# Reordering four places of a planned kernel: a conformer and state-space hybrid step on one Trainium2 core

## Chip, cores, metric

The kernel runs on one core of a Trainium2 chip. Times are device microseconds of one execution, from the first to the last work of the program; the median of several runs is compared. All arithmetic is in 32 bits.

## What is computed

One decoder layer for 2048 prompt tokens and 8 sample tokens, D = 1024. Cut to what the change bears on:

```
h = rmsnorm(x, g_pre);  proj = h @ w_in          # c_a c_b c_z | s_x s_z | g_c g_s
u = c_a * sigmoid(c_b);  v = causal_depthwise_conv(u, K=31)
v = silu(layernorm(v)) * silu(c_z);   y_c = v @ w_pc
ys = gelu(ssm(s_x));  ys = ys * sigmoid(ys @ w_glu + b_glu) * silu(s_z);  y_s = ys @ w_ps
o = (sigmoid(g_c) * y_c + sigmoid(g_s) * y_s) @ w_out
x1 = x + rmsnorm(o, g_post)
y = x1 + rmsnorm(p @ w_ple, g_ple) * sigmoid(x1 @ w_pg + b_pg)
```

The state-space branch (ssm) needs its discretisation first: dt = exp(log_dt) and exp(a_re * dt), for 128 x 16 parameters.

## The kernel before

Channels lie on the 128 partitions, tokens on the free axis. The tokens are worked in two halves: half 0 has 1032 columns (1024 prompt tokens and 8 samples, in blocks of 344), half 1 has 1024 (blocks of 512). A tile of a half is 128 channels; eight tiles are one activation.

Every product of a weight matrix is made of three matmuls: both operands are split into a high and a low part (names ending in h and l, for weights whi and wlo), and the products high-high, high-low and low-high are summed in one PSUM bank (`stages`, L310 to L312). The high part is a cast on ScalarE (L360, weights L263), the low part a subtraction on VectorE or GpSimd (L353). A weight chunk is 128 x 1024 and serves 128 to 512 outputs; its load (SP's queue, two raw buffers), cast and split (GpSimd) run one chunk ahead. The order of the chunks is the list `order` (L225 to L245).

A half goes through these stages (function `half`, L1142): s_x chunks; u chunks (c_b then c_a) with the gates in between; s_z; w_glu, evacuated by ScalarE's sigmoid; w_ps, whose result VectorE multiplies by the gate gs from DRAM; eight chunks of c_z (`act_to(z, AF.Silu)`, L1435); w_pc; w_out in two column parts; w_pg in two column parts. Beside them run tasks: the convolution on VectorE, partly on ScalarE and GpSimd; the state-space scans; the LayerNorm (`ln_task`, L1236); after w_glu the split of ys into ynh and ynl (`ysn_task`, L1394), which w_ps reads.

The order of instructions on each engine is fixed when the program is built. `Background` (L31) keeps an estimated clock for TensorE (`pe`) and for VectorE, ScalarE and GpSimd ("V", "S", "G"). A task is a generator: before each step it yields an engine and the time at which its operand is ready. `pump` emits the steps that may begin before `pe`: the earliest first, and the better priority (the lower number) among those within 0.05 us. An emitted step is one unit that the others can't enter, and `use` advances its engine's clock by its estimated cost. `drain` and `until` go on emitting beyond `pe` until a condition holds. A step on "P" (TensorE) counts as ready 1.2 us after its operand, a step on "Q" another MARGIN = 9.0 us later (L26, L60, L66).

The places that the change touches:

- `exp_dve` (L458): the exponential in 15 small VectorE operations of 128 x 16. `ssm_setup` (L475, priority 6) makes one copy, the first exponential, a product and the second, in one step that is booked with 11.0 us (L492 to L496). The tiles of h of the second column part of half 0 (`h_tile_task`, L724, from L1113, priority -1.7) become ready when `h_part`'s norm is done (L1106).
- `mean_task` (L369) and `norm_task` (L414): a column mean as a product with a matrix of 1/D. The sum is split (nh, nl), multiplied on TensorE (L385, L386) and evacuated by ScalarE (L396 or L398). `late=True` asks for "Q"; the LayerNorm's two calls (L1262, L1274) and `rms_task` (L1056) do so.
- the LayerNorm waits with its centring for `back_task` (L1188), which is added after w_ps (L1433) and loads six v tiles back from DRAM; `ln_out` (L1216) multiplies by cz and splits into vh and vl, which w_pc reads.
- `x1_tile` (L1515, priority -1): per tile a scale and an addition on VectorE, then `split_task` (L356): a cast on ScalarE (mh) and a low half (ml), which w_pg reads. A tile waits until the third before it is done. At w_out's evacuation L1552 drains the sum of squares of an older tile (`o_task`, L1504, priority 1).

Of the kernel before, what the change touches and what calls it, by code (L numbers as in the profile page):

```python
# [8 lines left out]
AF = mybir.ActivationFunctionType  # L9
# [4 lines left out]
P = 128  # L14
D = 1024
NT = 8
# [122 lines left out]
def build(nc, tc, A, O):  # L139
# [25 lines left out]
    with ExitStack() as ctx:  # L165
# [23 lines left out]
        def stt(out, a, s, b, op0, op1):  # L189
            V.scalar_tensor_tensor(out=out, in0=a, scalar=s, in1=b, op0=op0, op1=op1)  # L190
# [35 lines left out]
        for h in range(2):  # L226
            if h == 0:
                order += [("w_ple", j) for j in range(2)]
            if h == 0:
                for _ in range(2):  # L230
                    for c in range(EARLY):
                        order += [("w_in", CB + c), ("w_in", CA + c)]
            order += [("w_in", SX + b) for b in range(4)]
            gates = [("w_in", g + c) for g in (GC, GS) for c in range(8)]
            for c in range(0 if h else EARLY, 8):
                order += [("w_in", CB + c), ("w_in", CA + c)] + gates[:2]
                gates = gates[2:]
            order += gates
            order += [("w_in", SZ + b) for b in range(4)]
            order += [("w_glu", j) for j in range(2)]  # L240
            order += [("w_ps", j) for j in range(4)]
            order += [("w_in", CZ + c) for c in range(8)]
            order += [("w_pc", c) for c in range(8)]
            order += [("w_out", c) for c in range(8)] * 2
            order += [("w_pg", c) for c in range(8)] * 2  # L245
# [120 lines left out]
        def hilo(name):  # L366
            return alloc(F32R, name=name + "h"), alloc(F32R, name=name + "l")

        def mean_task(acc, blocks, bias, ready, k, split, late=False):  # L369

            yield from room(3 if split else k)
            if split:
                c = slice(blocks[0][0], blocks[-1][0] + blocks[-1][1])
                hl = hilo("n")
                ready = yield from split_task(acc, hl, c, "A", ready)
            else:
                out = [alloc(name="mean") for _ in range(k)]  # L380
            yield ("Q" if late else "P"), ready
            pts = [bank() for _ in blocks]
            for pt, (c0, n) in zip(pts, blocks):
                if split:
                    T.matmul(pt[:, 0:n], avgr, hl[0][:, c0:c0 + n], start=True, stop=False)  # L385
                    T.matmul(pt[:, 0:n], avgr, hl[1][:, c0:c0 + n], start=False, stop=True)  # L386
                else:
                    T.matmul(pt[:, 0:n], avg, acc[:, c0:c0 + n], start=True, stop=True)
                r = use("P", cP4(n) / 2 if split else cP4(n), ready)
            if split:  # L390
                free(*hl)
                out = [alloc(name="mean") for _ in range(k)]
            yield "S", r
            for pt, (c0, n) in zip(pts, blocks):
                if bias is None:
                    S.copy(out=out[0][:, c0:c0 + n], in_=pt[:, 0:n])  # L396
                else:
                    S.activation(out=out[0][:, c0:c0 + n], in_=pt[:, 0:n], func=AF.Identity, bias=bias)  # L398
                r = use("S", cS(n), r)
            return out, r  # L400
# [10 lines left out]
            tt(out, out, y)  # L411
            return use("V", 2 * cV(n) + cV2(n) + 0.3, r)

        def norm_task(acc, blocks, ready, split=False, late=False):  # L414

            c = slice(blocks[0][0], blocks[-1][0] + blocks[-1][1])
            (tmp, y), r = yield from mean_task(acc, blocks, epsc, ready, 2, split, late)
            r = yield from rstd_task(tmp[:, c], y[:, c], acc[:, c], c.stop - c.start, r)
            free(tmp, y)
            return r  # L420
# [37 lines left out]
        def exp_dve(out, x, w, ki):  # L458

            k, q = w  # L460
            ts(x, x, -87.0, 88.0, ALU.max, ALU.min)
            ts(k, x, 1.4426950408889634, MAGIC)
            ts(k, k, -MAGIC, None, ALU.add)
            stt(x, k, -0.693359375, x, ALU.mult, ALU.add)
            stt(x, k, 2.12194440e-4, x, ALU.mult, ALU.add)
            ts(q, x, 1.0 / 5040)
            for cf in (1.0 / 720, 1.0 / 120, 1.0 / 24, 1.0 / 6, 0.5, 1.0):
                stt(q, q, cf, x, ALU.add, ALU.mult)
            ts(q, q, 1.0, None, ALU.add)
            ts(ki, k, 127.0, 8388608.0, ALU.add, ALU.mult)  # L470
            tt(out, q, ki.bitcast(F32))

        tables = {"done": 0, "phases": 0}

        def ssm_setup():  # L475
# [14 lines left out]
            ki = par[:, 256:272].bitcast(I32)  # L490
            yield "V", 3.0
            ts(k3, ldt, 1.0)  # L492
            exp_dve(dt, k3, (k1, k2), ki)
            tt(th, are, dt)
            exp_dve(mag, th, (k1, k2), ki)
            r0 = use("V", 11.0, 3.0)  # L496
            yield "V", r0
            tt(th, aim, dt)
            ts(k1, th, 0.15915494309189535, MAGIC)
# [642 lines left out]
        def half(h, hT, finish):  # L1142
# [93 lines left out]
            def ln_task():  # L1236
                acc = None
                for c in range(NT):
                    while vs[c] is None or (h == 0 and seen[1] <= c):
                        yield None, bg.now + 0.5  # L1240
                    v, r = vs[c][0][:, PAD:PAD + n], vs[c][1]
                    if c == 0:
                        yield from room(1)
                        acc = alloc(name="acc")
                    e = bg.pick(n, r)
                    yield e, r
                    eng = GP if e == "G" else V
                    if h == 0:
                        eng.tensor_copy(out=v[:, HT:n], in_=vsm[:, c, :])
                        r = use(e, 0.1, r)  # L1250
                    if c == 0:
                        eng.tensor_copy(out=acc[:, full], in_=v)
                        r = use(e, cV(n) if e == "V" else cG(n), r)
                    else:
                        r = ew(e, acc[:, full], acc[:, full], v, ALU.add, n, r)
                    if c < NSPILL and not lnt["back"]:
                        yield None, r
                        dma(out=v_d[h][c * P:(c + 1) * P, 0:n], in_=v, after=r)
                        free(vs[c][0])
                        vs[c] = None  # L1260
                        lnt["out"].append(c)
                (mean,), r = yield from mean_task(acc, blocks, None, r, 1, True, True)  # L1262
                lnt["r"] = r
                lnt["sub"] = sub = []
                while not lnt["back"]:
                    yield None, bg.now + 0.5
                for c in range(NT):
                    while vs[c] is None:
                        yield None, bg.now + 0.3
                    sub.append(bg.add(ln_sub(c, mean, acc, r), 3.9 + 0.01 * c))  # L1270
                while not all(t[3] for t in sub):
                    yield None, bg.now + 0.2
                free(mean)
                r = yield from norm_task(acc, blocks, lnt["r"], True, True)  # L1274
                sub = [bg.add(ln_out(c, acc, r), 3.9 + 0.01 * c) for c in range(NT)]
                while not all(t[3] for t in sub):
                    yield None, bg.now + 0.2
                free(acc)
# [131 lines left out]
            def load_gs(j):  # L1410
                gl[j] = [unit("gs") for _ in range(2)]
                for m, t in enumerate(gl[j]):
                    dma(out=t[:, 0:n], in_=m2_d[h][(2 * j + m) * P:(2 * j + m + 1) * P, 0:n])

            load_gs(0)
            for j in range(4):
                if j == 0:
# [14 lines left out]
                free(*p)  # L1432
            bg.add(back_task(), 3.8)  # L1433

            for c in range(NT):  # L1435
                z = unit("cz")
                stage(("w_in", CZ + c), hT, blocks, act_to(z, AF.Silu))
                cz[c], zr[c] = z, bg.clock["S"] + 0.2
            for p in hT:
                free(*p)  # L1440
            bg.drain(ln)
# [73 lines left out]
            def x1_tile(k, c, cc, m, got):  # L1515
                while c > 2 and not x1s[k][c - 3][3]:
                    yield None, bg.now + 0.3
                yield from room(3)
                t = alloc(name="xr")
                rx = x_tile(h, c, t[:, 0:m], cc)  # L1520
                while not got:
                    yield None, bg.now + 0.2
                o, r = oT[c], got[0]
                yield "V", r
                stt(o[:, cc], o[:, cc], vcol("g_post", c), acc[:, cc], ALU.mult, ALU.mult)
                r = max(use("V", 0.15 + m / 560.0, r), rx)
                e = bg.pick(m, r)
                yield e, r
                r = ew(e, o[:, cc], o[:, cc], t[:, 0:m], ALU.add, m, r)
                free(t)  # L1530
                yield from split_task(o, x1T[c], cc, "A", r)

            def x1_task(k, r):
                c0, c1 = parts[k][0][0], parts[k][-1][0] + parts[k][-1][1]
# [171 lines left out]
```

## Time and profile before

| | us |
|---|---|
| median of 3 runs | 1971.6 |
| the runs | 1969.68, 1971.60, 1971.63 |
| profiled execution, its own time | 1969.63 |
| its span, first to last instruction | 1967.8 |
| TensorE busy | 1923.7 |
| VectorE busy | 1394.3 |
| GpSimd busy | 887.3 |
| ScalarE busy | 817.3 |

In the profile PE is TensorE's matmul, PEld its weight load, DVE VectorE, ACT ScalarE, POOL GpSimd, SP the queue of DMAs. L353 and the like are lines of the kernel; many operations go through one helper's line, so the names of tiles tell them apart. PEclk is the granted share of TensorE's clock. Times within the span count from the first instruction.

### The profile page before, as it was taken

How to read it: one execution, taken by the hardware profiler on the slowest of the kernel's cores; microseconds unless marked ns; L12 is line 12 of the kernel's file. 1: busy time of each engine (PE TensorE's matmuls, PEld its weight loads, DVE VectorE, ACT ScalarE, POOL GpSimd, SP SyncE). 2: the span in 40 equal slices, each digit the busy share in tenths (PEclk: the TensorE clock that was granted, in tenths of full speed). 3: DMA queues.
4: the chain of work that ended last, by engine and by line, in shares of the span. 5: the costliest groups of instructions: out<-in, count | busy, mean ns of one | idle time of the engine just before them, and what ended most of it. 6: DMA issues, size and time to landing. Idle time of an engine off the chain costs nothing. (4 is left out here: it accounts for less than half of the span.)

```text
span 1967.8 us, 27438 instructions
## 1 busy us (share of the span) xinstructions
PE 1923.7 (98%) x10772; PEld 1724.9 (88%) x10772; DVE 1394.3 (71%) x1490; ACT 817.3 (42%) x1362; POOL 887.3 (45%) x638
## 2 busy tenths in 40 slices
PE   8999999999999998999999999999999999999998
PEld 7899999999998998999997887888887788888786
DVE  6899978779988556425794488999984345641687
ACT  6533222245662353245542333344447335323552
POOL 1366534127672222244452424767767232224464
PEclk9899999999999999999999999999999999999999
DMA  8444455444315314324575445332221351432465
GB/s 315 142 132 140 159 168 193 172 138 154 116 46 185 139 51 143 117 77 133 185 226 177 165 143 176 116 108 86 86 75 57 122 200 53 160 107 80 136 207 166
DMA packets 111353, 273.10 MB, mean 139 GB/s; under 512 B 12648, under 2 KB 42472, under 8 KB 111208
## 3 DMA queue, kind: packets, MB, share of 16 engines
q1 hardware_dynamic: 110904, 271.16, 40.8%
q8 instruction: 84, 1.38, 0.3%
q14 instruction: 45, 0.37, 0.1%
q10 hardware_dynamic: 320, 0.20, 0.0%
HBM read 202.91 MB, written 69.36 MB: 138 GB/s over the span
## 5 line engine op out<-in xcount | busy, mean ns | idle before, releaser
L353 POOL TENSOR_TENSOR wlo<-raw,whi 128x512 fp32r<-128x512 f32 x386 | 556.7, 1461 | 949.9 <-ACT whi L263 946.2
L310 PE MATMUL bank<-hh,whi 128*128 128x344 f32 (+1 forms) x1888 | 664.2, 352 | 1.8 <-ACT hh L360 1.3
L311 PE MATMUL bank<-hl,whi 128*128 128x344 f32 (+1 forms) x1888 | 659.8, 349 | 2.8 <-DVE hl L353 2.7
L312 PE MATMUL bank<-hh,wlo 128*128 128x344 f32 (+1 forms) x1888 | 658.9, 349 | 1.4 <-POOL wlo L353 1.4
L190 DVE SCALAR_TENSOR_TENSOR acc<-u,prm,acc 128x1024 f32<-128x1024 f32 x392 | 504.7, 1288 | 10.7
L310 PEld LDWEIGHTS bank<-hh,whi 128*128 128x128 f32 x1888 | 355.7, 188 | 38.7 <-ACT hh L360 2.1
L311 PEld LDWEIGHTS bank<-hl,whi 128*128 128x128 f32 x1888 | 355.5, 188 | 35.8 <-DVE hl L353 4.4
L312 PEld LDWEIGHTS bank<-hh,wlo 128*128 128x128 f32 x1888 | 356.1, 189 | 34.9 <-POOL wlo L353 2.4
L263 ACT CAST whi<-raw 128x512 fp32r<-128x512 f32 x388 | 224.0, 619 | 195.0 <-PE bank L311 138.5
L310 PE MATMUL bank<-mh,whi 128*128 128x258 f32 (+1 forms) x768 | 247.7, 323 | 4.0 <-ACT whi L263 4.0
L312 PE MATMUL bank<-mh,wlo 128*128 128x258 f32 (+1 forms) x768 | 247.4, 322 | 3.7 <-POOL wlo L353 3.7
L311 PE MATMUL bank<-ml,whi 128*128 128x258 f32 (+1 forms) x768 | 246.5, 321 | 0.0
L353 POOL TENSOR_TENSOR ca<-ca,cq 128x512 f32<-128x512 f32 x144 | 196.3, 1391 | 30.6 <-ACT cq L944 30.6
L312 PEld LDWEIGHTS bank<-mh,wlo 128*128 128x128 f32 x768 | 146.2, 190 | 16.7 <-POOL wlo L353 5.7
L310 PEld LDWEIGHTS bank<-mh,whi 128*128 128x128 f32 x768 | 145.9, 190 | 16.5 <-ACT whi L263 5.3
L311 PEld LDWEIGHTS bank<-ml,whi 128*128 128x128 f32 x768 | 146.0, 190 | 11.6
L944 ACT ACTIVATE cq<-u,prm 128x512 f32<-128x512 f32 x144 | 101.3, 721 | 74.4 <-POOL ca L353 62.7
L310 PE MATMUL bank<-vh,whi 128*128 128x344 f32 (+1 forms) x320 | 112.5, 352 | 4.7 <-ACT vh L360 4.7
L311 PE MATMUL bank<-vl,whi 128*128 128x344 f32 (+1 forms) x320 | 113.1, 353 | 1.9 <-DVE vl L353 1.9
L344 ACT ACTIVATE gc<-bank 128x344 f32<-128x344 f32 (+1 forms) x80 | 41.0, 513 | 174.5 <-PE bank L312 172.1
L312 PE MATMUL bank<-vh,wlo 128*128 128x344 f32 (+1 forms) x320 | 112.4, 351 | 0.0
L353 DVE TENSOR_TENSOR oacc<-oacc,sq 128x258 f32<-128x258 f32 (+1 forms) x42 | 30.7, 746 | 100.0 <-ACT sq L1508 99.9
(221 smaller groups left out, 2494.7 us busy)
## 6 DMA issues: line engine op xcount, KB each, us to landing
raw<-in_w SPq DMA_DIRECT2D x194, 512.0 KB
cq<-cq SPq DMA_DIRECT2D x12, 512.0 KB
e<-e SPq DMA_DIRECT2D x8, 516.0 KB
rt<-e SPq DMA_DIRECT2D x8, 516.0 KB
gc<-gc SPq DMA_DIRECT2D x8, 516.0 KB
m<-gc SPq DMA_DIRECT2D x8, 516.0 KB
gs<-m SPq DMA_DIRECT2D x8, 516.0 KB
m<-gs SPq DMA_DIRECT2D x8, 516.0 KB
```

The source lines that it names most:

```text
L190: V.scalar_tensor_tensor(out=out, in0=a, scalar=s, in1=b, op0=op0, op1=op1)
L263: S.copy(out=hi, in_=t[:, c])
L310: T.matmul(o, hi[:, w], rh[:, c0:c0 + n], start=kt == 0, stop=False)
L311: T.matmul(o, hi[:, w], rl[:, c0:c0 + n], start=False, stop=False)
L312: T.matmul(o, lo[:, w], rh[:, c0:c0 + n], start=False, stop=kt == k - 1)
L344: S.activation(out=t[:, c0:c0 + n], in_=o, func=func)
L353: (V if e == "V" else GP).tensor_tensor(out=out, in0=a, in1=b, op=op)
L944: S.activation(out=q[:, h], in_=u[:, k + x * 512:k + x * 512 + 512], func=AF.Identity, scale=w(k))
```

## The change

It has four parts. (1) `exp_dve` becomes a generator with a yield after its fifth operation and booked costs of 2.0 and 3.0 us; `ssm_setup` yields once more between the two exponentials. (2) The chunk c_z 0 and its stage move from behind w_ps to between w_glu and w_ps; the other seven stay. (3) `late` takes a number as well: the LayerNorm's two products yield "P" with 1.5 us added to the time at which their operand is ready; `rms_task` keeps "Q". (4) In half 0 the cast of an x1 tile is yielded 3.0 us later.

```diff
             order += [("w_glu", j) for j in range(2)]
+            order += [("w_in", CZ + c) for c in range(1)]
             order += [("w_ps", j) for j in range(4)]
-            order += [("w_in", CZ + c) for c in range(8)]
+            order += [("w_in", CZ + c) for c in range(1, 8)]
...
-            yield ("Q" if late else "P"), ready
+            yield ("Q" if late is True else "P"), ready + (0.0 if late is True else late)
...
             stt(x, k, 2.12194440e-4, x, ALU.mult, ALU.add)
+            use("V", 2.0)
+            yield "V", 0.0
             ts(q, x, 1.0 / 5040)
...
             tt(out, q, ki.bitcast(F32))
+            use("V", 3.0)
...
-            exp_dve(dt, k3, (k1, k2), ki)
+            yield from exp_dve(dt, k3, (k1, k2), ki)
+            yield "V", 3.0
             tt(th, are, dt)
-            exp_dve(mag, th, (k1, k2), ki)
-            r0 = use("V", 11.0, 3.0)
+            yield from exp_dve(mag, th, (k1, k2), ki)
+            r0 = use("V", 0.5, 3.0)
...
-                (mean,), r = yield from mean_task(acc, blocks, None, r, 1, True, True)
+                (mean,), r = yield from mean_task(acc, blocks, None, r, 1, True, 1.5)
...
-                r = yield from norm_task(acc, blocks, lnt["r"], True, True)
+                r = yield from norm_task(acc, blocks, lnt["r"], True, 1.5)
...
+            def cz_chunk(c):
+                z = unit("cz")
+                stage(("w_in", CZ + c), hT, blocks, act_to(z, AF.Silu))
+                cz[c], zr[c] = z, bg.clock["S"] + 0.2
+
+            for c in range(1):
+                cz_chunk(c)
             load_gs(0)
...
-            for c in range(NT):
-                z = unit("cz")
-                stage(("w_in", CZ + c), hT, blocks, act_to(z, AF.Silu))
-                cz[c], zr[c] = z, bg.clock["S"] + 0.2
+            for c in range(1, NT):
+                cz_chunk(c)
...
-                yield from split_task(o, x1T[c], cc, "A", r)
+                yield from split_task(o, x1T[c], cc, "A", r + (3.0 if h == 0 else 0.0))
```

## Rows read from the trace of the kernel before

**Rows 1.** Page: the engines' busy time, and the costliest group of VectorE.

```profile
PE 1923.7 (98%) x10772; PEld 1724.9 (88%) x10772; DVE 1394.3 (71%) x1490; ACT 817.3 (42%) x1362; POOL 887.3 (45%) x638
...
L190 DVE SCALAR_TENSOR_TENSOR acc<-u,prm,acc 128x1024 f32<-128x1024 f32 x392 | 504.7, 1288 | 10.7
```

**Rows 2.** Waits of TensorE: who, for whom, us in total, times, longest.

```profile
PE bank L310 <- ACT whi L263: 11.8, 6, 7.3
```

**Rows 3.** Windows without a gap: length, PE busy (matmuls), PEclk, DMA share, GB/s.

```profile
970.00:981.00 11.00, 11.00 (x94) 1.00 0.54 171
700.00:711.00 11.00, 11.00 (x72) 1.00 0.16 48
1565.00:1576.00 11.00, 11.00 (x49) 1.00 0.75 258
```

**Rows 4.** Windows with gaps: length, busy of PE, PEld, DVE, ACT, POOL (instructions), PEclk, DMA.

```profile
74.00:88.00 14.00, 9.94 (x34) 7.41 (x33) 13.65 (x16) 6.99 (x10) 3.67 (x3) 0.63 0.21 79
596.00:607.00 11.00, 7.00 (x25) 5.41 (x24) 9.06 (x11) 5.38 (x7) 5.20 (x2) 0.69 0.52 192
743.00:757.00 14.00, 7.41 (x28) 5.60 (x27) 12.38 (x12) 7.96 (x9) 3.04 (x2) 0.76 0.20 77
923.00:934.50 11.50, 7.63 (x40) 7.13 (x39) 5.58 (x10) 5.33 (x14) 5.23 (x4) 0.70 0.19 56
...
1038.00:1051.00 13.00, 9.57 (x31) 6.91 (x31) 7.60 (x7) 3.49 (x5) 3.42 (x3) 0.74 0.73 232
...
1552.00:1560.00 8.00, 5.01 (x17) 2.65 (x17) 5.32 (x5) 5.50 (x7) 1.75 (x1) 1.00 0.76 263
```

**Rows 5.** VectorE's timeline at 57 to 86: start, us, engine, line, operation.

```profile
57.32 0.17 DVE L187 TENSOR_SCALAR spar<-prm 128x16 f32<-128x16 f32 x1
...
68.27 4.33 DVE L190 SCALAR_TENSOR_TENSOR xT<-xT,prm,acc 128x688 f32<-128x688 f32 x3
...
77.22 2.62 DVE L190 SCALAR_TENSOR_TENSOR xT<-xT,prm,acc 128x688 f32<-128x688 f32 x3
...
85.50 1.25 DVE L184 TENSOR_TENSOR spar<-prm,spar 128x16 f32<-128x16 f32 x1
```

**Rows 6.** Timelines of ScalarE and VectorE between w_glu and w_ps, half 0.

```profile
597.23 3.90 ACT L360 CAST ynh<-z 128x1032 fp32r<-128x1032 f32 x4
...
599.88 4.66 DVE L353 TENSOR_TENSOR ynl<-z,ynh 128x1032 fp32r<-128x1032 f32 x4
```

**Rows 7.** Timelines along the LayerNorm, half 0; the last two rows are half 1.

```profile
654.53 1.23 DVE L353 TENSOR_TENSOR nl<-acc,nh 128x1032 fp32r<-128x1032 f32 x1 [1.73 <-ACT nh L360]
...
668.58 1.14 ACT L396 COPY mean<-bank 128x344 f32<-128x344 f32 x3
...
693.71 1.23 DVE L353 TENSOR_TENSOR nl<-acc,nh 128x1032 fp32r<-128x1032 f32 x1 [1.12 <-ACT nh L360]
...
711.13 1.42 ACT L398 ACTIVATE mean<-bank,epsc 128x344 f32<-128x344 f32 x3
...
751.52 2.38 DVE L353 TENSOR_TENSOR vl<-cz,vh 128x1032 fp32r<-128x1032 f32 x2
...
1633.55 1.23 DVE L353 TENSOR_TENSOR nl<-acc,nh 128x1024 fp32r<-128x1024 f32 x1 [1.11 <-ACT nh L360]
...
1647.92 1.27 ACT L398 ACTIVATE mean<-bank,epsc 128x512 f32<-128x512 f32 x2
```

**Rows 8.** Timelines of ScalarE and VectorE, w_out's second part and w_pg, half 0.

```profile
919.20 0.62 ACT L360 CAST mh<-o 128x516 fp32r<-128x516 f32 x1 [3.24 <-DVE o L353]
...
926.67 1.14 ACT L263 CAST whi<-raw 128x512 fp32r<-128x512 f32 x2
...
945.93 0.48 ACT L346 ACTIVATE sgp<-bank,prm 128x258 f32<-128x258 f32 x1
...
986.85 0.69 DVE L353 TENSOR_TENSOR ml<-o,mh 128x516 fp32r<-128x516 f32 x1
...
989.66 0.48 ACT L346 ACTIVATE sgp<-bank,prm 128x258 f32<-128x258 f32 x1 [1.62 <-PE bank L312]
```

More of the change, by code (lines that the diff above doesn't have):

```diff
@@ L367, in hilo, with mean_task @@
             return alloc(F32R, name=name + "h"), alloc(F32R, name=name + "l")
-        def mean_task(acc, blocks, bias, ready, k, split, late=False):
+        def mean_task(acc, blocks, bias, ready, k, split, late=0.0):
             yield from room(3 if split else k)
@@ L412, in rstd_task, with norm_task @@
             return use("V", 2 * cV(n) + cV2(n) + 0.3, r)
-        def norm_task(acc, blocks, ready, split=False, late=False):
+        def norm_task(acc, blocks, ready, split=False, late=0.0):
             c = slice(blocks[0][0], blocks[-1][0] + blocks[-1][1])
```

## Prediction, made before the change was run

> **What bounds the kernel.** I read the engine shares first: TensorE is busy 98% of the span [rows 1], so time can only come out of its gaps. The list of what TensorE waits for is headed by casts of weights on ScalarE (whi) [rows 2]. Its idle time understates what a gap costs: in five of the six windows below the mean granted clock is only 0.63 to 0.76 [rows 4], so part of each runs at the lower of TensorE's two levels (1.2 instead of 2.4 GHz). So I count matmuls. At full rate an 11 us window holds 94 matmuls of 258 columns, 72 of 344 or 49 of 512, that is 0.117, 0.153 and 0.224 us each [rows 3]. The loss of a window is its length less its matmuls at that price:
>
> - first-half input, 74 to 88: 14.0 - 34 x 0.153 = 8.8 us;
> - first w_ps of half 0, 596 to 607: 11.0 - 25 x 0.153 = 7.2;
> - first w_pc of half 0, 743 to 757: 14.0 - 28 x 0.153 = 9.7;
> - w_out of half 0, second part, 923 to 934.5: 11.5 - 40 x 0.117 = 6.8;
> - first w_ps of half 1, 1552 to 1560: 8.0 - 17 x 0.224 = 4.2.
>
> That is 36.7 us, and each part of the change aims at one or two of these windows. The window 1038 to 1051 loses more than 6 us as well, but there the weight cast stands behind casts of the next half's input, which the change leaves alone.
>
> **Part 1, the exponential in two pieces.** Today VectorE starts the setup's small operations at 57.3, and the 16 operations (scale and low half) of the second input columns come only from 68.3 to 85.5 [rows 5]. In the planner these tiles have the better priority but become ready 0.2 us after VectorE falls free, and the exponential, booked as one block of 11 us, slips in. A first piece of 6 of the 32 operations is worth 11.0 x 6/32 = 2.1 us; after it the tiles win. They then start at 59.4. At the 0.87 us each of an undisturbed three they end at 73.3; at the 1.44 us of the first three, which ran beside GpSimd, they end at 82.4. TensorE arrives at about 74.3 and needs the last tile 7/8 of a block (24 x 0.153) later, at 77.5. So the loss left lies between 0 and 4.9 plus some slow clock; I take 1.5, since GpSimd does not split all the time. Gain 7.3 (range 2 to 8.8). The rest of the setup is not late for anyone: its next step already runs at 85.5, behind the same tiles.
>
> The Trainium skill, "SBUF — State Buffer", section "SBUF: two separate sides", says that VectorE and GpSimd share a port pair as an exclusive lock and that the loser waits for the whole instruction. By that rule the moved tiles pay for each split that runs beside them, and the gain would be nearer 2; the two scale rows agree on the direction.
>
> **Part 2, a z chunk ahead of w_ps.** w_ps needs four casts ynh (3.90 us on ScalarE from 597.2) and four ynl (4.66 us on VectorE, until 604.5) after the last sigmoid of w_glu [rows 6]. One z chunk needs only hT and is 72 x 0.153 = 11.0 us of TensorE in half 0 and 48 x 0.224 = 10.8 in half 1; both cover the losses of 7.2 and 4.2. What it adds: its evacuations queue behind ynh on ScalarE, with six PSUM banks to hold them; its weight load takes the place of w_ps 0 in SP's order, with no DMA more; the loads of gs are issued one chunk later in the code but still 3.7 us and more ahead of the first evacuation; the Silu table is loaded earlier, not more often, since w_ps has no ScalarE evacuation. If the y chain doesn't follow when TensorE comes 7.3 us earlier (part 1), the cover in half 0 is 11.0 - 7.3 = 3.7 and 3.5 us stay lost. I leave 1.0. Gain 10.4 (range 7.5 to 11.4).
>
> **Part 3, margin 1.5 instead of 9 for the LayerNorm's products.** In half 0 the sum's low half is ready at 655.8 and the mean is evacuated at 668.6; for the norm, 694.9 and 711.1 [rows 7]. That is 12.8 and 16.2 us for a few matmuls. With 7.5 us less each lands two blocks of 3.7 us earlier, so the chain gains 15 us. The last vl ends at 753.9, 9.7 us late in effect. But parts 1 and 2 bring TensorE to w_pc 7.3 + 6.2 = 13.5 us earlier, so the chain must move 23.2. It has the 15; some 5 more (an estimate: four convolution steps of 1.3 us [rows 1]), because VectorE has no evacuations during the moved z chunk and can take the last steps then; and its share of the 7.3, since the convolution follows TensorE's u tiles. What stays is the last z tile: evacuation, product, cast and split take about 4 us and TensorE needs them 3.2 us after it arrives. I leave 2.5 lost. Gain 7.2, with ends 9.7 and, if the chain doesn't move, a loss of 13.5. In half 1 nothing is lost there today; the norm's operand is ready at 1634.8 and the product is read at 1647.9 [rows 7]. Two blocks of 5.4 us earlier leaves next to no slack, so I book 0.7 us of new waiting on TensorE, with w_in matmuls queued behind it.
>
> **Part 4, casts of x1 later in half 0.** At 919.2 ScalarE stands 3.24 us before a cast of x1 that waits for VectorE, more such casts follow, and the weight cast that TensorE needs comes only at 926.7 [rows 8]. The reason is in the planner: the evacuation of w_out waits (L1552) for an older tile's sum of squares, whose VectorE step loses to x1 tiles of better priority, so the x1 casts are all written into ScalarE's order before that wait is over. With 3.0 us between sum and cast, VectorE's plan gets holes, the sum of squares fits in, and the weight cast goes ahead. Ends: 0 (the order stays) and 6.8 (all of it); I take 4.8, nearer the upper end because the casts themselves aren't urgent: w_pg evacuates its first block at 945.9, so it needs part 0 from about 943, some 17 us after the last of them. For part 1 the last ml ends at 987.5, and the second part of w_pg begins when the sixteenth block of the first is evacuated, at 989.7 [rows 8], so 3 us later costs about 1.0.
>
> **Sum.** 7.3 + 10.4 + 7.2 + 4.8 = 29.7, less 0.7 and 1.0, is 28.0. The profiled execution took 1969.6 us (span 1967.8), the lowest of the runs shown; the median is 1971.6. 1969.6 - 28.0 = 1941.6; I forecast 1942.5, half of the distance to the median included.
>
> **The rivals.**
> - *Handed back at w_pc.* VectorE, not the margin, sets the LayerNorm chain: the 13.5 us of parts 1 and 2 return as a longer wait for vh, and part 3 is worth nothing. 28.0 - 7.2 - 13.5 = 7.3: 1964. For it: VectorE is busy 12.4 of 14 us at that wait [rows 4]. Against: in the 12.8 and 16.2 us before the means it is the product that is awaited, not VectorE.
> - *The x1 order stays* (part 4 doesn't do what it says): 1942.5 + 4.8 = 1947.
> - *Tiles beside GpSimd at 1.44 us each*, the lock of the skill's SBUF page as a mechanism: 4.9 us and 2 of slow clock stay, 5.4 more than I left: 1948.
> - *Slower.* The 3.0 us become real delays one after another: ScalarE and VectorE work in order, a tile starts only when the third before it is done, and if every cast blocks the next tile's operations, eight tiles are 24 us late. Part 0 has 17 us of room, part 1 only 2; the stalls are then 7 and 22 us, with 3.4 of slow clock each, 36 in all: 1978. It outweighs the gains from about 2.6 us of real delay a tile. Against: the tiles are independent, three in flight.
>
> **Chances.** Forecast case (1930 to 1950 without the next two) 0.60, x1 order 0.13, lock 0.08, handed back 0.14, slower 0.05. Faster or slower by 0.2% (4 us, about what repeats can tell) means below 1967.7 or above 1975.5. A handed-back case a little worse than worked out falls inside: same 0.05. The range goes from 1930 (all 36.7 us and some of the window at 1038) to 1962, which cuts off most of handed-back, the slower case and little else.
>
> **What the new profile would show.** Part 1: hl by about 78 and the clock at 1.0 around 77. Part 2: no idle before the first ynh in either half. Part 3: means evacuated within about 5 and 9 us of their operands in half 0, and a loss under 4 us before w_pc. Part 4: no wait for whi in w_out's second part. The forecast is wrong if w_pc of half 0 still waits over 8 us, or if a product of the norm becomes a wait of TensorE above 3 us.

## The result, and the profile after

The changed kernel takes 1948.8 us (median of 4 runs, 1947.5 to 1950.4); the kernel before, run beside it on the same chip, 1970.6. The ratio is 0.9891, 95% interval 0.9874 to 0.9909: faster by 21.9 us, where 28 were forecast. The profiled execution took 1947.7 us (span 1945.8).

TensorE's line of the page, as in [rows 1]:

```profile
PE 1913.9 (98%) x10772; PEld 1719.7 (88%) x10772; DVE 1410.7 (73%) x1486; ACT 818.5 (42%) x1362; POOL 912.6 (47%) x642
```

The share of TensorE is the same, and its busy time for the same matmuls fell by 9.8 us, since less of it ran at the lower clock: the granted clock of the whole execution is 0.996 on average, before 0.990. What moved is seen in the windows, with the columns of [rows 4]; each stretch is where the same stage now stands (196 to 207 and 972 to 983 are new):

```profile
74.00:88.00 14.00, 10.09 (x39) 8.21 (x39) 12.76 (x23) 6.41 (x11) 6.44 (x4) 0.79 0.47 164
196.00:207.00 11.00, 7.64 (x49) 7.02 (x48) 10.76 (x10) 8.23 (x19) 9.11 (x5) 0.84 0.43 138
605.00:616.00 11.00, 11.00 (x72) 11.00 (x72) 9.97 (x10) 5.79 (x10) 5.58 (x4) 1.00 0.42 144
743.00:757.00 14.00, 13.30 (x85) 13.01 (x84) 7.60 (x11) 4.24 (x8) 5.98 (x4) 1.00 0.37 127
915.00:926.50 11.50, 11.50 (x98) 11.50 (x98) 10.10 (x13) 6.08 (x15) 6.80 (x4) 1.00 0.25 67
972.00:983.00 11.00, 7.12 (x45) 6.70 (x45) 10.79 (x14) 2.65 (x6) 3.71 (x2) 0.85 0.69 200
1020.00:1033.00 13.00, 11.42 (x67) 9.71 (x66) 10.57 (x9) 5.03 (x7) 6.43 (x4) 1.00 0.82 265
1543.00:1551.00 8.00, 8.00 (x36) 6.49 (x35) 0.69 (x1) 1.63 (x3) 2.75 (x3) 1.00 0.83 314
```

At the prediction's prices for a matmul, w_ps loses nothing in either half (72 x 0.153 = 11.0 and 36 x 0.224 = 8.1), w_pc of half 0 loses 14.0 - 85 x 0.153 = 1.0 instead of 9.7, and w_out nothing. The first-half input loses 14.0 - 39 x 0.153 = 8.0 instead of 8.8: part 1 did next to nothing there. Two losses are new. In the second part of w_pg half 0 it is 11.0 - 45 x 0.117 = 5.7 us. At 196 to 207, where matmuls of several kinds run, TensorE stands 3.4 us, and the clock falls to its lower level behind it. The window that took the place of 1038 to 1051, which the prediction said the change leaves alone, now holds 67 matmuls at full clock instead of 31 at 0.74. Matmuls of 258 and of 512 columns run there; each kind at its price, some 2 us are lost where before lost 7.

The waits of TensorE behind the two new losses (who, for whom, us in total, times, longest):

```profile
PE bank L312 <- DVE ml L354: 3.9, 2, 3.3
PE bank L782 <- ACT gc L345: 3.4, 1, 3.4
```

### The profile page after: what moved, and what is told of

Read it like the earlier page. It is cut to its first block, busy times and chain, and to the rows that moved or that the text cites. A ratio compares the mean times of both kernels' runs of the same rounds, so it can differ in the third digit from the quotient of the medians.

```text
span 1945.8 us, 27443 instructions
## 1 busy us (share of the span) xinstructions
PE 1913.9 (98%) x10772; PEld 1719.7 (88%) x10772; DVE 1410.7 (73%) x1486; ACT 818.5 (42%) x1362; POOL 912.6 (47%) x642
## 4 chain that ended last, share of the span: by engine, by line
PE 80%; DVE 8%; issue 3%; POOL 2%; DMA 1%; ACT 1%; SPq 0%; POOLq 0%; DVEq 0%; ACTq 0%
PE bank L311 25%; PE bank L313 25%; PE bank L312 25%; DVE acc L190 2%; PE bank L842 2%; POOL wlo L354 1%; PE bank L845 1%; DVE sgp L354 1%; PE bank L782 1%; DVE e L190 1%; DVE o L354 0%; DVE hl L354 0%; DVE ml L354 0%; DMA v<-v 0%; DVE gw L184 0%
## 5 line engine op out<-in xcount | busy, mean ns | idle before, releaser
L354 POOL TENSOR_TENSOR wlo<-raw,whi 128x512 fp32r<-128x512 f32 x386 | 571.5, 1499 | 896.6 <-ACT whi L264 893.2
L311 PEld LDWEIGHTS bank<-mh,whi 128*128 128x128 f32 x768 | 145.4, 189 | 12.1 <-ACT whi L264 1.0
```

Source lines behind the costliest of these rows:

```text
L311: T.matmul(o, hi[:, w], rh[:, c0:c0 + n], start=kt == 0, stop=False)
L354: (V if e == "V" else GP).tensor_tensor(out=out, in0=a, in1=b, op=op)
```

## The experiments

Twelve kernels ran, each beside the kernel before on the same chip. Ratios are to that kernel, with their 95% intervals.

| run | edit | median us | ratio |
|---|---|---|---|
| after | all four parts | 1948.8 | 0.9891 (0.9874 to 0.9909) |
| e1_exp_whole | after, part 1 undone | 1940.7 | 0.9853 (0.9838 to 0.9867) |
| e4_z_back | after, part 2 undone | 1957.2 | 0.9940 (0.9923 to 0.9957) |
| e3_ln_margin_off | after, part 3 undone | 1966.0 | 0.9975 (0.9966 to 0.9984) |
| e2_x1_first_part | after, part 4 in the first column part only | 1949.1 | 0.9897 (0.9882 to 0.9912) |
| e8_exp_alone | before, part 1 alone | 1976.0 | 1.0038 (1.0024 to 1.0052) |
| e7_x1_alone | before, part 4 alone | 1960.9 | 0.9951 (0.9938 to 0.9963) |
| e5_memset_vector | after, memsets on VectorE | 1946.4 | 0.9886 (0.9872 to 0.9899) |
| e12_setup_late | e1, setup some 10 us later | 1947.3 | 0.9884 (0.9868 to 0.9901) |
| e13_no_exp | e1, no exponentials | 1940.0 | 0.9851 (0.9836 to 0.9866) |
| e11_exp_early | e9, setup started early | 1943.2 | 0.9865 (0.9848 to 0.9881) |
| e9_x1_half | e1, delay 3.0 and 1.5 | 1937.8 | 0.9841 (0.9828 to 0.9855) |
| e10_x1_four | e1, four x1 tiles in flight | 1941.1 | 0.9856 (0.9841 to 0.9872) |

### Part 1 undone, and part 1 alone

```
-            use("V", 2.0)
-            yield "V", 0.0
...
-            yield from exp_dve(dt, k3, (k1, k2), ki)
-            yield "V", 3.0
+            exp_dve(dt, k3, (k1, k2), ki)
...
-            yield from exp_dve(mag, th, (k1, k2), ki)
-            r0 = use("V", 0.5, 3.0)
+            exp_dve(mag, th, (k1, k2), ki)
+            r0 = use("V", 11.0, 3.0)
```

> The changed kernel with part 1 undone: the exponential again one block, booked 11 us. Theory: the split moved the tiles ahead but ScalarE is held from 59.2 to 65.5 (a DMA on its queue, a table load), so the window 74 to 88 loses about 8.5 us with or without it, while the later setup makes a new loss of 5.9 us at 196 to 205. Without the split: 74 to 88 still loses 8 to 10, nothing is lost at 196, and the time falls by 4 to 6 us, to about 1943. Rival (the forecast's term): the split is worth 7.3 us, so without it 1956. Second rival: the loss at 196 is not the split's, then it stays and the time is within 2 us of 1949.

The other way round, the same lines put into the kernel before:

> The kernel before with part 1 alone (exponential in two pieces). Theory: no gain at 74 to 88, the setup some 8 us later, a new loss of about 6 us at 196 to 205, and nothing of it won back later: 1975 to 1979, slower than before. Rival: before's later waits (w_ps, w_pc) absorb the lateness, since TensorE comes later there: 1970 to 1972. Second rival, the forecast's term: 1963.

Undone, the time falls to 1940.7, by 8.0 us and 2 more than the theory's range; alone, it rises by 6.5 (1976.0 against 1969.5). So the term that was forecast as a gain of 7.3 is a loss of 6.5 to 8, in either surrounding. Windows of the kernel after without part 1, then the second of them with part 1 alone:

```profile
73.00:87.00 14.00, 8.89 (x30) 6.53 (x29) 13.96 (x17) 7.01 (x10) 3.71 (x3) 0.66 0.22 76
196.00:207.00 11.00, 11.00 (x77) 11.00 (x76) 10.77 (x9) 4.96 (x12) 8.47 (x6) 1.00 0.44 137
```

```profile
196.00:207.00 11.00, 7.64 (x49) 7.03 (x49) 10.76 (x10) 8.14 (x19) 9.20 (x5) 0.84 0.44 141
```

With the block whole the input window loses 14.0 - 30 x 0.153 = 9.4 us, with the split 8.0 (above), and the loss at 196 is there with the split only.

The start times of the same matmuls in two profiles show where the time goes. With the block whole against the changed kernel, about 5 us are gained by 425, at the loss of 196. Another 2 us come little by little between 1160 and 1880, where no single stretch stands out: the matmuls of 512 columns start 231.25 ns apart on average there, in the changed kernel 232.13, both at full clock. That accounts for what the theory's range lacks; what sets this interval is not shown. With part 1 alone 4.8 us are lost by 425, and 2.2 of them come back at the wait of w_ps, as the rival in that expectation has it in part.

### Why the window at 74 to 88 doesn't close

The tiles do go first now: VectorE starts them at 57.5 instead of 68.3 [rows 5]. But ScalarE is not ready for them. Its timeline in the changed kernel (start, us, engine, line, operation, idle time before it and its releaser):

```profile
62.40 0.34 ACTq L490 DMA_DIRECT2D dtile<-in_ssm_d  x1
62.84 1.28 ACT L345 ACT_TABLE_LOAD   x1 [3.66 <-POOL sfin L489]
...
65.52 2.10 ACT L361 CAST hh<-xT 128x688 fp32r<-128x688 f32 x3
```

A DMA issued from ScalarE's queue waits for a memset on GpSimd, which stands behind weight splits; the casts of the tiles wait until 65.5, behind the DMA until 62.8 and then behind a table load, a gate and two weight casts, and VectorE idles 5.2 us for them. Moving the memsets tests the DMA's part:

```
-            GP.memset(dtile, 0.0)
-            GP.memset(sfin, 0.0)
+            V.memset(dtile, 0.0)
+            V.memset(sfin, 0.0)
```

> The changed kernel (exponential in two pieces) with the memsets of dtile and sfin on VectorE instead of GpSimd, so that ScalarE's queue no longer stands 3.7 us before a DMA that waits for GpSimd. Theory: VectorE's 5.2 us of idle time after the first three tiles come from that hold, and the whole setup runs late for the same reason; then hh comes some 3 us earlier, the window 74 to 88 loses 5 to 6 instead of 8.5, and the loss at 196 to 205 shrinks or goes: 1940 to 1946. Rival: the tiles are held by VectorE's own rate and by GpSimd's splits of the weights (wlo) that TensorE then waits for; the time stays within 2 us of 1949.

The median is 1946.4, 2.4 us lower, but the ratios are 0.9886 and 0.9891 with intervals that overlap, and the two profiled executions took 1948.1 and 1947.7: a gain is not shown. Its windows are

```profile
73.00:87.00 14.00, 10.62 (x43) 9.82 (x44) 12.72 (x24) 6.29 (x10) 6.42 (x4) 0.76 0.48 164
196.00:207.00 11.00, 7.64 (x42) 7.13 (x41) 10.75 (x10) 7.47 (x18) 9.84 (x5) 0.69 0.41 133
```

7.4 us are lost in the first, and the second is worse than it was (42 matmuls for 49). ScalarE's wait only shrank from 3.7 to 2.3 us, now for another transfer:

```profile
61.77 1.28 ACT L345 ACT_TABLE_LOAD   x1 [2.33 <-DMA e<-e]
```

So the memsets on GpSimd cost ScalarE 1.3 us, and the window closes by 0.6. What the whole hold is worth this run doesn't show.

The sharper question is what the window would be with no exponential at all:

```
-            exp_dve(dt, k3, (k1, k2), ki)
+            ts(dt, k3, 0.0, 0.01)
             tt(th, are, dt)
-            exp_dve(mag, th, (k1, k2), ki)
-            r0 = use("V", 11.0, 3.0)
+            ts(mag, th, 0.0, 0.9)
+            r0 = use("V", 1.0, 3.0)
```

> The 1940.7 us version with both exponentials left out (constants in their place, 2 operations for 32, booked 1 us instead of 11); it leaves out that part of the computation. It shows what the window 73 to 87 is worth at most when the tiles come first and the setup is early too. Theory A (a real wait, wholly to be had): 9 to 10 us go at 73 to 87, nothing appears later, 1930 to 1932. Theory B (the time is set later by the state's chain around 195, as the version with the exponential started early suggests): part of it goes at 73 to 87 and comes out again before 205, and the time is 1936 to 1941.

The time is Theory B's (1940.0), but its reason is not seen: nothing comes out again before 205. The loss simply never leaves. The window at 74 to 88 of that kernel and the ten us ahead of it:

```profile
64.00:74.00 10.00, 8.42 (x43) 7.86 (x42) 8.78 (x8) 6.76 (x13) 7.42 (x5) 0.83 0.33 99
74.00:88.00 14.00, 10.66 (x53) 9.54 (x52) 13.41 (x34) 8.00 (x12) 6.86 (x4) 0.88 0.54 184
```

10.0 - 43 x 0.153 = 3.4 and 14.0 - 53 x 0.153 = 5.9, together 9.3 us, with ten us of VectorE's work taken out ahead of it; with the exponentials the same 24 us hold 88 matmuls and lose 10.5. ScalarE's hold is still there (3.55 us), so the run shows what the window loses without the exponentials, not without both. Where the ten us went is in VectorE's groups by line at 55 to 90 (times x | busy us, mean ns | idle before). Before, after, and without exponentials:

```profile
L190 DVE SCALAR_TENSOR_TENSOR xT<-xT,prm,acc 128x688 f32<-128x688 f32 x8 | 8.7, 1137 | 0.0
L353 DVE TENSOR_TENSOR hl<-xT,hh 128x688 fp32r<-128x688 f32 x8 | 6.7, 882 | 0.0
```

```profile
L190 DVE SCALAR_TENSOR_TENSOR xT<-xT,prm,acc 128x688 f32<-128x688 f32 x8 | 10.2, 1311 | 0.0
L354 DVE TENSOR_TENSOR hl<-xT,hh 128x688 fp32r<-128x688 f32 x8 | 9.2, 1179 | 6.0 <-ACT hh L361 6.0
```

```profile
L190 DVE SCALAR_TENSOR_TENSOR xT<-xT,prm,acc 128x688 f32<-128x688 f32 x8 | 12.3, 1575 | 0.0
L354 DVE TENSOR_TENSOR hl<-xT,hh 128x688 fp32r<-128x688 f32 x8 | 9.9, 1277 | 3.6 <-ACT hh L361 3.6
```

The same 16 operations take 15.4, 19.4 and 22.2 us. The earlier they run, the more of them stand beside GpSimd's weight splits: 3.6, 12.1 and 16.4 us of that time by the timelines. Two timelines of the last kernel, VectorE's and GpSimd's, show the price:

```profile
64.20 0.93 DVE L190 SCALAR_TENSOR_TENSOR xT<-xT,prm,acc 128x688 f32<-128x688 f32 x1
...
69.59 3.82 DVE L190 SCALAR_TENSOR_TENSOR xT<-xT,prm,acc 128x688 f32<-128x688 f32 x2
...
65.78 6.90 POOL L354 TENSOR_TENSOR wlo<-raw,whi 128x512 fp32r<-128x512 f32 x4 [3.53 <-ACT whi L264]
```

One tile takes 0.93 us while GpSimd waits, and the next two 1.91 each beside a run of splits. The Trainium skill ("SBUF — State Buffer", "SBUF: two separate sides") names a port pair that VectorE and GpSimd share as a lock; the trace agrees, at twice the time for this operation.

So the input window is held by tiles, splits and casts together; their shares are not separated. Taking the exponential out of their way gives VectorE time that it spends beside GpSimd (4.0 us more for the tiles in the changed kernel) and behind ScalarE (6.0 us idle). The prediction's 0.87 us each was the price of tiles that run later, when GpSimd is idle.

### What the loss at 196 is

ScalarE's timeline in the changed kernel, and in the same kernel without part 1:

```profile
192.00 1.07 ACT L580 ACTIVATE ph<-ph 128x1024 f32<-128x1024 f32 x1 [7.67 <-POOL ph L354]
...
199.69 0.81 ACT L345 ACTIVATE gc<-bank 128x344 f32<-128x344 f32 x2
...
201.03 0.66 ACT L673 COPY we<-bank 128x512 f32<-128x512 f32 x1
```

```profile
184.70 0.59 ACT L669 COPY we<-bank 128x512 f32<-128x512 f32 x1
...
189.47 1.06 ACT L576 ACTIVATE ph<-ph 128x1024 f32<-128x1024 f32 x1 [3.09 <-POOL ph L354]
...
197.15 0.81 ACT L345 ACTIVATE gc<-bank 128x344 f32<-128x344 f32 x2
```

Both have a block of activations for the state's phases (ph), and the evacuation of a gate (gc) behind it. Without the split, a state's evacuation (we) stands ahead of that block; with it, the block comes first and 2.5 us later, and TensorE stands for a PSUM bank until gc is evacuated from 199.7 on. The prediction's sentence that the rest of the setup "is not late for anyone" was the wrong one. Lateness by itself was tried with two exponentials more on scratch values right behind the tiles:

```
+            for _ in range(2):
+                exp_dve(k3, k3, (k1, k2), ki)
             tt(th, aim, dt)
```

> The 1940.7 us version (changed kernel with the exponential whole) with two exponentials more on scratch values in VectorE's order, not booked in the planner, right behind the tiles of the second columns: some 10 us by which the setup comes later in fact than in the plan, with everything ahead of it as it was. Theory: the loss at 196 to 205 of the changed kernel is this lateness, so it appears here too, 4 to 6 us, the window 73 to 87 stays at 9 to 10, and the time is 1944 to 1947. Rival: the setup has room for it and the loss in the changed kernel came from another order of ScalarE's work: 1940 to 1942.

The time came out at the upper end of the theory's (1947.3, 6.6 us more), but at another place than expected. Windows, and GpSimd's timeline:

```profile
107.00:118.00 11.00, 7.90 (x34) 7.62 (x33) 7.08 (x12) 1.48 (x3) 10.96 (x20) 0.69 0.32 94
196.00:207.00 11.00, 11.00 (x82) 10.63 (x81) 10.75 (x10) 9.64 (x15) 7.87 (x5) 1.00 0.31 97
```

```profile
105.45 3.49 POOL L627 COPY pwr<-pw 128x16 f32<-128x16 f32 x16 [1.41 <-DVE pw L184]
...
109.06 5.83 POOL L354 TENSOR_TENSOR wlo<-raw,whi 128x512 fp32r<-128x512 f32 x4
```

A late setup is dear, then, but here because GpSimd's copies of the powers wait for VectorE and the weight splits stand behind them. At 196 nothing is lost, with the state's evacuations ahead of the phases as without the split. That doesn't clear lateness: the phases start at 197.3, 7.8 us later than without the two exponentials, but TensorE is 7.9 us later by then too, so nothing is late against it there. For the order speaks the kernel with the setup started early (below): its phases start at 184.2, some 5 us earlier as TensorE is, the evacuations of the state stand behind them again, and TensorE stands 2.6 us. So the order goes with a loss where nothing is late; how much of the 3.4 us in the changed kernel comes from the 2.5 us of lateness is open. That the order changed because the planner takes the split to gain its time at 74 to 88, and places what follows accordingly, is argued, not shown.

### Parts 2 and 3

```
-            order += [("w_in", CZ + c) for c in range(1)]
...
-            for c in range(1):
-                cz_chunk(c)
...
```

> The changed kernel with part 2 undone: all z chunks behind w_ps again. Theory: the two waits of w_ps return, 7.2 us in half 0 and 4.2 in half 1, 11.4 in all, and w_pc wins back the 1.0 it loses now: 1959 to 1961. Rival: half 0's 7.2 us were only moved on to w_pc in the kernel before, and the LayerNorm now has room, so half of them is won back there: 1955 to 1957.

1957.2: 8.4 us for part 2, between the two, next to the rival's 1957. The waits of w_ps are back in its windows, 11.0 - 34 x 0.153 = 5.8 and 8.0 - 17 x 0.224 = 4.2 us:

```profile
600.00:611.00 11.00, 7.77 (x34) 6.33 (x33) 8.00 (x9) 5.43 (x8) 3.61 (x2) 0.84 0.50 192
1538.00:1546.00 8.00, 5.52 (x17) 3.85 (x16) 5.33 (x5) 5.50 (x7) 2.12 (x1) 0.79 0.74 263
```

The rival's reason isn't seen: w_pc of half 0 holds the same 85 matmuls in 14 us (742 to 756) as in the changed kernel. It is the wait of w_ps in half 0 that is smaller than the 7.2 us of the kernel before.

```
-                (mean,), r = yield from mean_task(acc, blocks, None, r, 1, True, 1.5)
+                (mean,), r = yield from mean_task(acc, blocks, None, r, 1, True, True)
...
-                r = yield from norm_task(acc, blocks, lnt["r"], True, 1.5)
+                r = yield from norm_task(acc, blocks, lnt["r"], True, True)
```

> The changed kernel with part 3 undone: the LayerNorm's two products placed with the old rule again. Theory: the margin carries w_pc of half 0. The chain of sum, mean, norm, output then ends where it did before (or earlier by the 7.2 us by which TensorE comes earlier), so w_pc of half 0 waits 10 to 17 us, and the time is 1959 to 1966. Rival: the margin only shifts the chain inside slack that VectorE's freed time gave; then less than 3 us are lost and the time is 1949 to 1952.

1966.0, 17.2 us: the theory's upper end, but in two places. Windows at w_pc of half 0 and of half 1:

```profile
742.00:756.00 14.00, 7.45 (x30) 5.97 (x29) 9.34 (x9) 5.75 (x7) 3.04 (x2) 0.76 0.24 83
1679.00:1693.00 14.00, 8.24 (x22) 4.84 (x22) 9.78 (x9) 6.54 (x9) 3.02 (x2) 0.78 0.13 51
```

14.0 - 30 x 0.153 = 9.4 us, and 14.0 - 22 x 0.224 = 9.1. The second did not exist before: as I read it, with the old margin the z chunk moved away from w_pc takes the cover from the LayerNorm of half 1. Part 2 without part 3 then gives its gain back there, so the parts can't be added up one by one; no run leaves out both to compare it with.

In the kernel after, the mean of half 0 and its operand, and the norm's, answer to [rows 7]:

```profile
655.00 1.15 ACT L397 COPY mean<-bank 128x344 f32<-128x344 f32 x3 [6.42 <-PE bank L387]
690.96 1.43 ACT L399 ACTIVATE mean<-bank,epsc 128x344 f32<-128x344 f32 x3 [0.81 <-PE bank L387]
```

```profile
649.43 1.22 DVE L354 TENSOR_TENSOR nl<-acc,nh 128x1032 fp32r<-128x1032 f32 x1
688.00 2.37 DVE L354 TENSOR_TENSOR nl<-acc,nh 128x1032 fp32r<-128x1032 f32 x1 [1.12 <-ACT nh L361]
```

655.00 - 650.65 = 4.4 us instead of 12.8, and 0.6 instead of 16.2. The norm's product now comes before its operand; TensorE waits 0.6 us for it.

### Part 4

```
-                yield from split_task(o, x1T[c], cc, "A", r)
+                yield from split_task(o, x1T[c], cc, "A", r + (3.0 if h == 0 else 0.0))
```

> The kernel before with part 4 alone (3.0 us between sum and cast of x1 in half 0). Theory: it removes the 6.8 us at 923 to 934 and some 8 of the 10 us at 1006 to 1050, and adds 5.9 at the second part of w_pg: net about 9, so 1961 against 1970. Rival (the forecast's view of part 4): 4.8 less 1.0 is 3.8, so 1966, and the 8 us at 1006 to 1050 come from parts 2 and 3 or from TensorE's earlier arrival.

1960.9: 10.2 us, as the theory had it. Its windows show the three pieces: w_out's second part is full (99 matmuls at 915 to 926.5), the second part of w_pg loses 11.0 - 47 x 0.117 = 5.5 us (980 to 991), and the end of w_pg loses about 1 us (1027 to 1040) where before lost 7. What it does at the end of w_pg is seen in what ScalarE waits for there (us in total, times, longest), in the kernel before at 1000 to 1050, and with part 4 alone at 993 to 1040:

```profile
ACT hh L360 <- DVE xn L190: 26.4, 6, 6.3
```

```profile
ACT hh L360 <- DVE xn L190: 8.5, 4, 2.5
```

The casts of the next half's input stood in ScalarE's order well ahead of their data, and weight casts waited behind them. With the x1 casts later they are placed nearer to it. Which column part does that was asked by

```
-                yield from split_task(o, x1T[c], cc, "A", r + (3.0 if h == 0 else 0.0))
+                yield from split_task(o, x1T[c], cc, "A", r + (3.0 if h == 0 and k == 0 else 0.0))
```

> The changed kernel with the 3.0 us between sum and cast only in the first column part of half 0; the second part's casts are placed as before. Theory: the loss of 5.9 us at 974 to 983 (TensorE waits for the low half ml of x1's second part) goes, the losses at 1006 to 1050 stay gone (they hang on the casts of the first part or on the general order), so about 1943. Rival: the smaller loss at 1006 to 1050 (1.9 us where before lost some 10) comes from the same later casts of the second part and returns: 1943 + 8 = 1951. Second rival: the loss at 974 has another cause (VectorE behind by other work) and stays: 1949.

The rival's mechanism holds, and the time (1949.1) is 2 us below its 1951. 972 to 983 is full (94 matmuls), but the last stretch of w_pg is not, as its window and ScalarE's wait at 985 to 1032 show:

```profile
1021.00:1032.00 11.00, 7.32 (x24) 5.23 (x23) 6.62 (x7) 3.49 (x5) 2.68 (x2) 0.84 0.68 214
```

```profile
ACT hh L361 <- DVE xn L190: 25.0, 6, 5.5
```

The delay of the second part costs 5.7 us in w_pg and takes away the waits at its end; without it neither is so, and the time is the same within the measurement. It asks for a middle:

```
-                yield from split_task(o, x1T[c], cc, "A", r + (3.0 if h == 0 else 0.0))
+                yield from split_task(o, x1T[c], cc, "A", r + ((3.0, 1.5)[k] if h == 0 else 0.0))
```

> The changed kernel with the exponential whole again and the delay of the x1 casts 3.0 us in the first column part, 1.5 in the second. Theory: the loss of 5.9 us at 970 to 979 comes from how late the last x1 tiles of the second part start (each may start only when the third before it is done, and the outputs of w_pg take VectorE in between); half the delay moves the last tiles some 3 us earlier, enough to take away half of it or more, and the later order stays: 1935 to 1938, against 1940.7. Rival: as with no delay at all in the second part, the loss comes out at 988 to 1030 instead: 1941 or more.

1937.8, as expected, and the fastest of all: 11.0 us below the changed kernel, the intervals of the ratios apart. Against the 1940.7 it started from it is 2.9 us; there the runs don't overlap (1936.5 to 1939.1 and 1939.8 to 1941.1), but the intervals of the ratios do. It keeps both windows nearly full:

```profile
967.00:978.00 11.00, 11.00 (x95) 11.00 (x94) 10.77 (x12) 3.53 (x7) 4.84 (x5) 1.00 0.64 202
1012.00:1023.00 11.00, 10.26 (x59) 8.48 (x60) 10.86 (x8) 3.05 (x5) 7.33 (x4) 1.00 0.79 257
```

The other way to the same end was more tiles in flight:

```
-                while c > 2 and not x1s[k][c - 3][3]:
+                while c > (2, 3)[k] and not x1s[k][c - (3, 4)[k]][3]:
```

> The changed kernel with the exponential whole again and, in the second column part of x1, four tiles in flight instead of three (a tile may start when the fourth before it is done), the delay of 3.0 us kept in both. Theory: the loss at 970 to 979 is the tile chain; with four in flight the last tiles start one step (about 3 us) earlier and most of the 5.9 us goes: 1935 to 1938. Rival: VectorE's other work decides when the last tiles run; the loss stays: 1940 to 1942.

The loss at w_pg goes (94 matmuls at 967 to 978), so the tile chain was its cause. But 1012 to 1023 has 9.15 us of busy TensorE where the run above has 10.26, and the time, 1941.1 with runs from 1936.6 to 1944.1, can't be told from the 1940.7 it started from.

### An attempt on the input window

VectorE idles 7.1 us at 47 to 54, ahead of the tiles. The setup was started before the embedding's matmuls, so that the first exponential fills that hole and the second follows the tiles:

```
+            yield None, 43.0
             yield from room(4)
...
-            yield "V", 3.0
+            yield "V", 46.0
             ts(k3, ldt, 1.0)
             exp_dve(dt, k3, (k1, k2), ki)
+            use("V", 5.5)
+            yield "V", 62.0
             tt(th, are, dt)
...
+            bg.add(ssm_setup(), 6)
             embed(wait)
-            bg.add(ssm_setup(), 6)
```

> The 1937.8 us version (exponential whole, delay of x1 casts 3.0 and 1.5) with the state setup started before the embedding's matmuls instead of after them: the first of the two exponentials goes into VectorE's 7.1 us of idle time at 47.4 to 54.5, where it waits for the mean, and the second comes after the tiles of the second input columns. Theory: the tiles then start at 58 to 60 as with the split, but the setup is not late and ScalarE is not held by the DMA, so of the 9 to 10 us at 73 to 87 some 5 to 9 go and no loss appears at 196: 1929 to 1933. Rival: VectorE idles after the first tiles as in the changed kernel, since ScalarE's casts set the pace, the second exponential is late again and a loss at 196 returns: 1936 to 1941.

1943.2, worse than both had it. The input window is nearly mended, 14.0 - 72 x 0.153 = 3.0 us lost at full clock, but some comes back at 188 to 199 with the same wait for gc as in the changed kernel:

```profile
74.00:88.00 14.00, 11.78 (x72) 11.28 (x73) 13.00 (x35) 5.44 (x9) 8.28 (x6) 1.00 0.42 152
188.00:199.00 11.00, 8.41 (x63) 7.74 (x62) 10.75 (x10) 8.24 (x19) 7.23 (x4) 1.00 0.17 49
```

```profile
PE bank L781 <- ACT gc L345: 2.6, 1, 2.6
```

The window is not mended by the filled hole alone: VectorE starts the tiles at 53.3, 4.2 us earlier than in the changed kernel; ScalarE's DMA is issued at 46.5 with nothing to wait for, so its first cast comes at 57.7 instead of 65.5; and two of the eight low halves run on GpSimd. Which of these counts most is not separated. Against its base, the start times of the matmuls show 6 us gained by 86; 2.5 are lost again at 88 to 107, where TensorE waits 1.9 us for a weight split, and the rest by 207. Some 3 us are then lost up to 1030, most of it at the end of w_pg, and nearly 2 little by little in half 1.

## Why the prediction was right, and where it was wrong

The sign, the case (faster by more than 0.2%) and the range were right; the time came 6.3 us above the forecast. That it came so near is in part luck: part 1 was wrong by some 14 us or more, and parts 3 and 4 were worth more than forecast.

- **Part 1 (7.3, ends 2 to 8.8): wrong in sign.** It costs 8.0 us in the changed kernel and 6.5 alone. Two steps failed: the price of the tiles (0.87 us each "since GpSimd does not split all the time"; they took 1.31 and 1.18 on average, and waited 6.0 us for ScalarE), and the setup that "is not late for anyone" (TensorE waits 3.4 us at 196). Of the two signs that the prediction gave for it one failed: the last low half ends at 83.3, not by 78. The clock is at its full level around 77 as foreseen, but falls to the lower one at 82. The lower end of 2 left out a loss for no reason that the rows gave. The rival beside GpSimd's lock had the first mechanism, and its 1948 agrees with the result by accident: it knew nothing of the loss at 196 or at w_pg.
- **Part 2 (10.4): mechanism right.** Both waits of w_ps are gone; undone it costs 8.4, by two waits of 5.8 and 4.2.
- **Part 3 (7.2): mechanism right, too small.** w_pc of half 0 keeps 1.0 lost where 2.5 were left. The two products gained 8.4 and 15.6 us where 15 in all were booked, and TensorE came to w_pc 1.3 us earlier instead of 13.5, mostly because part 1 lost what it was to gain. That half 1 would need the margin as well, once part 2 takes a z chunk from it, was missed: 17.2 for the part undone. Without part 3 the kernel comes to 1966.0, near the 1964 of the "handed back" rival, but half of that loss is in half 1, which the rival did not have.
- **Part 4 (4.8): too small.** w_out's second part is mended whole (6.8). The step "the change leaves alone" for 1038 to 1051 failed: the same delay reorders the casts of the next half's input. Against it, the 1.0 booked for the second part of w_pg was 5.7, of the kind of the "slower" rival: each x1 tile waits for the third before it, and the outputs of w_pg take VectorE in between. Alone the part is worth 10.2 net, where 3.8 were booked.

## What to carry to other kernels

Work moved earlier on an engine keeps its price only if its neighbours there are the same: look at what the other engines do at the new time, not at the old, and take a duration from a row with that neighbour. A stall that has one visible cause may have three engines just behind it; leaving the suspected work out altogether shows quickly what moving it can bring at most. And a delay in one stage's casts is also a change of order for the next stage, whose waits have to be read too before it is called untouched.

## What the runs showed of the hardware that was not expected

The 16 tile operations on VectorE cost 15.4, 19.4 or 22.2 us by how much of them ran beside GpSimd's splits, a single one 0.93 or 1.91 us. A DMA that is issued from ScalarE's queue and waits for a memset holds what stands behind it on ScalarE: it idled 3.66 us, and still 2.33 us, for another transfer, with the memset moved. At full clock, the matmuls of 512 columns in half 1 start 231.2 to 232.2 ns apart on average from kernel to kernel, in one profile of each; over some 3000 of them that is up to 2.8 us, with the cause open.
